# Moving the last conditioning groups of a two-layer encoder from the K/V projections into the first feed-forward

## The chip, the cores and the metric

The kernel runs on one core of one Trainium2 chip. The metric is device time: microseconds from the start of the program on the core to its end. The chip has five engines that run their own instruction streams in order and meet at semaphores: TensorE (PE) multiplies matrices, VectorE (DVE) and GpSimd (POOL) do elementwise work and reductions, ScalarE (ACT) does activations, casts and copies, SyncE (SP) mainly starts DMAs. DMAs move data between the chip's memory and the on-chip buffer.

## The reference

The program is a trunk of two layers over one sequence of 1024 tokens with 1024 channels, everything in float32. Each layer has a mixer and a SwiGLU feed-forward; the first mixer is a gated short convolution, the second is forgetting attention over a shared K/V set. A vector `c` conditions every sub-layer:

```
c_act = silu(c)
for l in 0, 1:
    sh1, sc1, g1, sh2, sc2, g2 = split(c_act @ w_ada[l] + b_ada[l], 6)
    h = x * (1 + sc1) + sh1
    y = short_conv_mixer(h)                     # layer 0
    # layer 1: k, v, gates = shared_kv(x, c, w_ada_kv, b_ada_kv)   (2 more vectors of c)
    #          y = forgetting_attention(h, w_q, k, v, gates, w_o)
    x = layer_norm(alpha * x + g1 * y)
    h = x * (1 + sc2) + sh2
    y = (silu(h @ w_gate) * (h @ w_up)) @ w_down       # inner width 2816
    x = layer_norm(alpha * x + g2 * y)
```

So 14 conditioning vectors of 1024 numbers are needed: six of each layer and two for K and V. Each is the product of one vector with a 1024 by 1024 matrix. The matrices hold some 59 MB.

## The kernel before

**Precision and tiles.** Every large product is made of three passes on PE: a float32 operand is split into a rounded high part (ACT, a cast) and the rest (DVE, a subtraction), and high x high, high x low and low x high are added up (`mm3`, lines 169 to 171). A pass is one matmul of a 128 by 128 weight tile with a 128 by 512 tile.

**The conditioning groups.** A vector is computed in two groups of 512 columns, 24 groups without the first two vectors, which are done at the start. A group needs 1024 rows by 512 columns of weights. DVE adds them up, one step for 128 rows: the first step is a multiplication (`ada_step`, line 260), the other seven multiply and add into one accumulator `ga` (line 262). Then PE transposes the accumulator in four pieces (`ada_finish`, line 285), DVE reduces them (line 287) and adds the bias (line 278). The work is done at three places:

- 8 groups during the convolution (`ada_pump`, weights by POOL's DMA queue).
- 10 groups during the first feed-forward's first phase (`ada_lq`, `ada_slot`). A group is cut into *quarters*: one DMA of 512 KB by SP's queue (line 763) into a page of the common pool, and two DVE steps. One quarter is done in each slot (below).
- 6 groups beside the K and V projections (`ada_item`). Again in quarters; the DMA is issued by POOL (line 807), into the one page lent for it, and an item first does the quarter that was loaded and then asks for the next. What is left after the last K product is done in a loop before the Q products start (`while self.adaq or self.adan or self.adap`).

**The feed-forward's first phase** (`hidden`) computes silu(h w_gate) * (h w_up) with seven products M1 to M7 instead of eight for each pair of 128-column blocks (a fast matrix multiplication of two by two blocks). A *slot* is one such product: 24 matmuls on PE. Sums of weight blocks that M5, M3 and M7 need are made by POOL (lines 898 to 903). In a slot the next slot's weights are split (ACT line 639, DVE line 640), the product runs, and its two banks are evacuated by DVE and ACT (lines 942, 957 to 988), which also forms the inputs of the second phase and stores them.

There are 77 slots in the first phase: slots 0 to 11 are M1 and M2 of pairs 0 to 5, and lie beside the end of a layer norm; from slot 12 on the other five products of pairs 0 to 5 follow, five slots a pair (*early pairs*); from about slot 41 pairs 6 to 10 follow with seven slots each (*late pairs*). Evacuating an early pair adds a part that was put aside in memory, so DVE has more to do there.

**What sets the order.** Loads stand in one list in the order of use (`queue`), and are started from its head while more than a reserve of pages of the common pool is free (`lq_pump`; the reserve is 5 pages there). The call `queue(2, len(slots), ...)` in `run` puts one quarter of conditioning weights behind the blocks of each slot `i >= nada`, with `nada = nfirst + ADA0` and `nfirst = 12`. `adaq_lq(n)` takes `n` groups for that and leaves the others to `ada_item`. The loop in `run` calls `ada_slot` after each slot `i >= nada`. A scheduler then sets the order of instructions on each engine from this; instructions of one engine may change places where the data allow it.

Before the change `ADA0` is 22, so quarters begin in slot 34, and 10 groups, 40 quarters, fill slots 34 to 73.

Of the kernel before, what the change touches and what calls it, by code (L numbers as in the profile page):

```python
# [77 lines left out]
class Builder:  # L78
# [734 lines left out]
    def hidden(self, l, nearly, left):  # L813
# [7 lines left out]
        slots = [(j, n) for j in early for n in ("M1", "M2")]  # L821
        nfirst = len(slots)
        nada = nfirst + ADA0
        late = None
# [27 lines left out]
        def m1_load(j):  # L852
            def fn():
                pg = self.fpage()
                nc.sync.dma_start(pg.rearrange("p a b -> p (a b)"), self.dr["m1"][j * P:(j + 1) * P])
                return pg
            self.lq_add(("m1", j), fn)

        def b11_load(j):
            def fn():  # L860
                pg = self.fpage()
                nc.sync.dma_start(pg[:, 0], self.dr["M1"][j * P:(j + 1) * P])
                return pg
            self.lq_add(("b11", j), fn)
# [3 lines left out]
        def queue(lo, hi, ada):  # L868

            for i in range(lo, hi):  # L870
                for q in [look + i] if i else range(look + 1):
                    if q < len(slots):
                        j, n = slots[q]
                        load(("e" if j in early and n in ("M1", "M2") else "", j, *src[n]))
                if i + look + 1 < len(slots):
                    j, n = slots[i + look + 1]
                    for b in needs.get(n, ()):
                        load(("", j, *b))
                j, n = slots[i]
                if j in early and n == "M5":  # L880
                    m1_load(j)
                if j in early and n == "M3":
                    b11_load(j)
                if i >= nada and ada:
                    self.lq.append(ada.pop(0))
            assert not ada

        def load(key):
            if key not in queued:
                queued.add(key)  # L890
                self.blocks_load(l, key[1], [key[2:]], key[0])
# [167 lines left out]
        def steps(i):  # L1059
            def begin():  # L1060
                self.slot = i
                ahead(i)
            out = [begin]
            if i < nfirst:
                out.append(lambda: self.lq_pump(FRES + 3 * self.sums_left))
            for m in range(2):
                out += [lambda m=m: product(i, m), lambda m=m: evac(i, m)]
            return out + [lambda: self.flush(i)]
# [5 lines left out]
                parts(i)  # L1074

        def run(beside, before_end):
            queue(2, len(slots), self.adaq_lq(len(self.adaq) - 6) if l == 0 else [])
            self.down_queue()
            first = [f for i in range(nfirst) for f in steps(i)]
            self.weave((first, 0.0, 1.0), (beside, *LNE))  # L1080
            for i in range(nfirst, len(slots)):
                self.lq_pump(FRUN if i < len(slots) - 12 else FRUN + 2)
                if i == len(slots) - 2:
                    before_end()
                for f in steps(i):
                    f()
                if i >= nada and l == 0:
                    self.ada_slot()
            self.flush()
            assert not self.adal  # L1090
# [932 lines left out]
FRUN = 5  # L2023
FDOWN = 18
LNE = (0.05, 1.0)
ADA0 = 22
LOOK = 1
FILL = (0,)*5+(2,)*4+(1,)*16
QB_ORDER = (6, 7, 0, 1, 2, 3, 4, 5)
# [33 lines left out]
```

## Time and profile before

| | us |
|---|---|
| median of 3 runs | 2443.26 (2442.11 to 2446.3) |
| the profiled execution | 2442.01 |
| its span in the profile | 2440.2 |
| PE busy in the span | 2320.7 (95%) |
| DVE busy | 1767.6 (72%) |
| POOL busy | 814.3 (33%) |
| first feed-forward, first phase, slots 12 to 73 | 495.5 to 837 |
| K, V, gates, first half of Q | about 1081 to 1342 |

The profile counts the time in which an engine executes. Matmul ends are modelled and matmuls overlap, so a row of PE that is busy all the time says that it never waited; how fast it went is read from the count of matmuls and the granted clock (PEclk: 1.00 is 2.4 GHz, 0.5 would be 1.2 GHz). Times in the windows are microseconds from the start of the span. The views name code by its line (L262 is line 262) and tiles by their names: `ga` is the accumulator of a group, `pg` any page of the pool, `mm` and `sm` banks for results of PE, `tA` and `tB` short-lived tiles.

### The profile page before, as it was taken

The page shows a single profiled execution, that of the slowest core. Times are in us where ns is not written, and L with a number is a line of the kernel's source. Part 1 is how long each engine was busy: PE and PEld are TensorE (multiplying, and loading weights), DVE is VectorE, ACT ScalarE, POOL GpSimd, SP SyncE. Part 2 cuts the span into 40 slices and gives each one's busy share as a digit, 9 for nine tenths or more (in the row PEclk, how much of TensorE's full clock was granted, in tenths as well). Part 3 has the DMA queues.
Part 4 walks back from the last instruction along what each step waited for, and adds up shares of the span by engine and source line. Part 5 has one row for each costly group of instructions (what it writes and reads, how often), then busy time and mean ns, then how long its engine had stood idle before and what let it go on. Part 6 is the DMA issues. An engine that isn't in the chain of part 4 may idle for free. (4 is left out here: it accounts for less than half of the span.)

```text
span 2440.2 us, 29980 instructions
## 1 busy us (share of the span) xinstructions
PE 2320.7 (95%) x10629; PEld 1885.4 (77%) x10629; DVE 1767.6 (72%) x2382; ACT 929.6 (38%) x1423; POOL 814.3 (33%) x664
## 2 busy tenths in 40 slices
PE   7899999999999899999989999999999999999987
PEld 5688887788888788777777777777778888878876
DVE  6665548988988878986474567888787865577973
ACT  3311113622233343434222566666462233333432
POOL 6411003343222323343100465565443322231314
PEclk9999999999999999999999999999999999999998
DMA  8343213555666855115658565563374443374401
GB/s 277 96 129 121 87 36 112 182 185 172 225 198 211 301 173 167 58 52 198 193 183 241 157 189 153 134 161 97 104 244 156 160 130 117 116 272 134 164 1 69
DMA packets 322762, 375.42 MB, mean 154 GB/s; under 512 B 20053, under 2 KB 214821, under 8 KB 322613
## 3 DMA queue, kind: packets, MB, share of 16 engines
q1 hardware_dynamic: 302260, 318.25, 42.1%
q0 software_dynamic: 8736, 29.89, 4.0%
q10 hardware_dynamic: 11616, 25.37, 2.8%
q8 instruction: 84, 1.38, 0.2%
q14 instruction: 66, 0.53, 0.1%
HBM read 288.83 MB, written 84.61 MB: 153 GB/s over the span
## 5 line engine op out<-in xcount | busy, mean ns | idle before, releaser
L169 PE MATMUL mm<-pg,pg 128*128 128x512 f32 x2872 | 1138.7, 398 | 36.3 <-DVE pg L1306 11.1
L170 PE MATMUL mm<-pg,pg 128*128 128x512 f32 x2872 | 1133.3, 395 | 8.5 <-DVE pg L373 6.9
L171 PE MATMUL mm<-pg,pg 128*128 128x512 f32 x2872 | 1130.6, 394 | 6.2 <-POOL pg L371 4.0
L169 PEld LDWEIGHTS mm<-pg,pg 128*128 128x128 f32 x2872 | 546.8, 190 | 158.0 <-DVE pg L1306 14.8
L170 PEld LDWEIGHTS mm<-pg,pg 128*128 128x128 f32 x2872 | 546.7, 190 | 123.6 <-DVE pg L373 10.0
L171 PEld LDWEIGHTS mm<-pg,pg 128*128 128x128 f32 x2872 | 545.9, 190 | 123.2 <-POOL pg L371 5.3
L640 DVE TENSOR_TENSOR pg<-pg,pg 128x1024 fp32r<-128x1024 f32 (+1 forms) x322 | 464.7, 1453 | 96.4 <-ACT pg L639 51.4
L639 ACT CAST pg<-pg 128x1024 fp32r<-128x1024 f32 (+1 forms) x322 | 320.1, 1013 | 515.4 <-PE mm L171 163.6
L1174 POOL TENSOR_TENSOR pg<-pg,pg 128x1024 f32<-128x1024 f32 (+1 forms) x48 | 121.9, 2547 | 271.6 <-DVE pg L640 125.1
L1306 DVE SCALAR_TENSOR_TENSOR pg<-mm,mods,pg 128x512 f32<-128x512 f32 x184 | 134.8, 744 | 60.9 <-PE mm L171 60.7
L159 ACT CAST pg<-pg 128x1024 fp32r<-128x1024 f32 x78 | 81.5, 1052 | 210.5 <-PE mm L170 147.5
L1725 POOL TENSOR_SCALAR pg<-pg,st 128x512 f32<-128x512 f32 (+7 forms) x128 | 97.7, 772 | 116.7 <-DVE st L1723 108.9
L262 DVE SCALAR_TENSOR_TENSOR ga<-pg,cact,ga 128x512 f32<-128x512 f32 x112 | 95.4, 852 | 43.1 <-DMA pg<-in_w_ada_dram 39.1
L1748 DVE TENSOR_TENSOR pg<-sm,pg 128x512 fp32r<-128x512 f32 x192 | 104.0, 550 | 24.2 <-ACT pg L1747 21.3
L901 POOL TENSOR_TENSOR pg<-pg,pg 128x1024 f32<-128x1024 f32 x22 | 55.9, 2540 | 172.4 <-DMA pg<-in_ffn_w_up_dram 93.6
L960 ACT ACTIVATE tA<-tA 128x512 f32<-128x512 f32 x66 | 41.7, 631 | 184.3 <-DVE tA L959 184.3
L1747 ACT CAST pg<-sm 128x512 fp32r<-128x512 f32 x192 | 89.1, 480 | 49.2 <-PE sm L1744 45.6
L1722 ACT ACTIVATE pg<-s,st 128x512 f32<-128x512 f32 (+7 forms) x128 | 94.5, 744 | 28.8 <-DVE st L1719 19.2
L316 POOL DMA_DIRECT2D g<-in_w_ada_dram x64 | 34.8, 543 | 204.9 <-DVE ga L262 76.5
L1716 DVE TENSOR_REDUCE st<-s 128x1 f32<-128x1024 f32 (+3 forms) x96 | 91.2, 951 | 15.2 <-PE s L1710 14.5
L163 DVE TENSOR_TENSOR pg<-pg,pg 128x1024 fp32r<-128x1024 f32 x58 | 72.5, 1257 | 40.0 <-ACT pg L159 39.2
L898 POOL TENSOR_TENSOR pg<-pg,pg 128x1024 f32<-128x1024 f32 x22 | 54.6, 2484 | 139.8 <-DMA pg<-in_ffn_w_up_dram 106.3
(217 smaller groups left out, 2542.4 us busy)
## 6 DMA issues: line engine op xcount, KB each, us to landing
scr_hid<-pg SPq DMA_DIRECT2D x154, 256.0 KB
pg<-scr_hid SPq DMA_DIRECT2D x70, 512.0 KB
pg<-in_ffn_w_gate_dram SPq DMA_DIRECT2D x112, 256.0 KB
pg<-in_ffn_w_up_dram SPq DMA_DIRECT2D x112, 256.0 KB
pg<-in_ffn_w_down_dram SPq DMA_DIRECT2D x88, 256.0 KB
pg<-in_w_ada_dram SPq DMA_DIRECT2D x40, 512.0 KB
g<-in_w_ada_dram POOLq DMA_DIRECT2D x64, 256.0 KB, 3.1
pg<-in_conv_w_in_dram SPq DMA_DIRECT2D x24, 512.0 KB
```

Source lines behind the costliest of these rows:

```text
L169: mm(out, lhsT=whi, rhs=xhi, start=first, stop=False, skip_group_check=skip)
L170: mm(out, lhsT=whi, rhs=xlo, start=False, stop=False, skip_group_check=skip)
L171: mm(out, lhsT=wlo, rhs=xhi, start=False, stop=last, skip_group_check=skip)
L262: eng.scalar_tensor_tensor(acc, w, s, acc, op0=ALU.mult, op1=ALU.add)
L639: nc.scalar.copy(hi[:, 0:n], flat[:, 0:n])
L640: nc.vector.tensor_tensor(lo[:, 0:n], flat[:, 0:n], hi[:, 0:n], op=ALU.subtract)
L1174: tt = lambda o, a, b, op=ALU.subtract: gp.tensor_tensor(o, a, b, op=op)
L1306: nc.vector.scalar_tensor_tensor(z, bank, gate[:, k:k + 1], z, op0=ALU.mult, op1=ALU.add)
L1716: nc.vector.tensor_reduce(m, p[:, :, 0:n], axis=AX.X, op=ALU.min)
L1722: nc.scalar.activation(lg[:, i], p[:, i, 0:n], AF.Exp, bias=m[:, i:i + 1], scale=-1.0, accum_out=s[:, i:i + 1])
L1725: nc.gpsimd.tensor_scalar(lg[:, i], lg[:, i], s[:, i:i + 1], 1.0, op0=ALU.mult, op1=ALU.mult)
L1748: nc.vector.tensor_tensor(pt[:, 1, a:], p[:, a:], pt[:, 0, a:], op=ALU.subtract)
```

## The change

The list of the first phase takes all groups that are left, 16 instead of 10, and quarters begin in slot 12 instead of slot 34. So 64 quarters lie in slots 12 to 75, and the last group is finished in slot 76. No group is left for `ada_item`: its calls beside K and V find nothing to do, and the loop before the Q products is empty.

```diff
@@ hidden(), run @@
         def run(beside, before_end):
-            queue(2, len(slots), self.adaq_lq(len(self.adaq) - 6) if l == 0 else [])
+            queue(2, len(slots), self.adaq_lq(len(self.adaq)) if l == 0 else [])
             self.down_queue()
@@ constants @@
 LNE = (0.05, 1.0)
-ADA0 = 22
+ADA0 = 0
 LOOK = 1
```

Each number of instructions stays: 24 DMAs of 512 KB go from POOL's queue to SP's, and 48 DVE steps, 24 transposes, 6 reductions and 6 bias additions move from the K/V stage to the first phase. All quarters from the first one on stand 22 slots earlier than they did.

On DVE, in the middle of an early pair of the first phase (the end of M7, then M5 and M4), the order before is this; no conditioning step stands there:

```order
L959 TENSOR_TENSOR tA_4184<-mm_700_4091,pg_4029 128x512
L979 TENSOR_TENSOR pg_4199<-mm_702_4106,pg_4029 128x512
L980 TENSOR_TENSOR pg_4199<-pg_4199,tA_4184 128x512
L640 TENSOR_TENSOR pg_4246<-pg_4122,pg_4245 128x1024
L988 TENSOR_TENSOR pg_4199<-pg_4199,pg_4083 128x512
L942 TENSOR_TENSOR pg_4226<-mm_718_4213,pg_4125 128x512
L988 TENSOR_TENSOR pg_4083<-pg_4199,pg_4083 128x512
L942 TENSOR_TENSOR pg_4226<-mm_720_4228,pg_4125 128x512
L640 TENSOR_TENSOR pg_4283<-pg_4008,pg_4282 128x1024
L959 TENSOR_TENSOR tA_4262<-mm_700_4091,pg_3928 128x512
```

At the same place of another early pair the change has this order:

```order
L942 TENSOR_TENSOR pg_4305<-mm_739_4292,pg_4239 128x512
L988 TENSOR_TENSOR pg_4274<-pg_4274,pg_4185 128x512
L262 SCALAR_TENSOR_TENSOR ga_4233<-pg_4241,cact_99,ga_4233 128x512
L988 TENSOR_TENSOR pg_4185<-pg_4274,pg_4185 128x512
L942 TENSOR_TENSOR pg_4305<-mm_741_4307,pg_4239 128x512
L262 SCALAR_TENSOR_TENSOR ga_4233<-pg_4241,cact_99,ga_4233 128x512
L640 TENSOR_TENSOR pg_4327<-pg_4236,pg_4326 128x1024
L262 SCALAR_TENSOR_TENSOR ga_4233<-pg_4282,cact_99,ga_4233 128x512
L959 TENSOR_TENSOR tA_4343<-mm_716_4152,pg_4006 128x512
L262 SCALAR_TENSOR_TENSOR ga_4233<-pg_4282,cact_99,ga_4233 128x512
L640 TENSOR_TENSOR pg_4372<-pg_4141,pg_4371 128x1024
L979 TENSOR_TENSOR pg_4274<-mm_718_4167,pg_4006 128x512
```

Two conditioning steps a slot now stand between the evacuations (L942, L959, L979, L988) and the splits that the next products need (L640).

On DVE at the end of the K products the order before has the last group's steps between the evacuations of K (L1483) and the modulated input of Q (L369, L373):

```order
L163 TENSOR_TENSOR pg_9460<-pg_9457,pg_9459 128x1024
L1483 TENSOR_TENSOR tB_9448<-mm_1573_9422,tA_9447 128x512
L262 SCALAR_TENSOR_TENSOR ga_9356<-pg_9420,cact_99,ga_9356 128x512 x2
L1483 TENSOR_TENSOR tB_9489<-mm_1580_9463,tA_9488 128x512
L262 SCALAR_TENSOR_TENSOR ga_9356<-pg_9455,cact_99,ga_9356 128x512 x2
L287 TENSOR_REDUCE mods_101<-sm_9527 128x4
L1483 TENSOR_TENSOR tB_9522<-mm_1583_9496,tA_9521 128x512
L278 SCALAR_TENSOR_TENSOR mods_101<-mods_101,bada_192 128x4
L369 TENSOR_SCALAR tB_9536<-pg_6172,v_1499_9003,mods_101 128x512
```

With the change the same place reads:

```order
L163 TENSOR_TENSOR pg_9469<-pg_9466,pg_9468 128x1024
L1483 TENSOR_TENSOR tB_9461<-mm_1575_9435,tA_9460 128x512
L1483 TENSOR_TENSOR tB_9498<-mm_1581_9472,tA_9497 128x512
L1787 CAST mask_9583<-tA_9578 128x128
L1483 TENSOR_TENSOR tB_9529<-mm_1584_9503,tA_9528 128x512
L369 TENSOR_SCALAR tB_9536<-pg_6304,v_1514_9068,mods_101 128x512
```

The steps, the reduction and the bias are gone there, and the cast of attention's mask has moved up.

## Rows read from the trace of the kernel before

**Rows 1.** PE's waits from 1075 to 1300: total us, times, longest.

```profile
PE sm L285 <- DVE ga L262: 13.2, 4, 4.6
...
PE sm L1577 <- DVE pg L1570: 3.4, 1, 3.4
```

**Rows 2.** Stretches, K/V stage: busy us of PE, PEld, DVE, ACT, POOL; PEclk.

```profile
1130.00:1180.00 50.00, 48.60 (x219) 39.97 (x218) 22.00 (x31) 11.66 (x16) 4.19 (x6) 1.00 0.65 204
1198.00:1208.00 10.00, 7.14 (x28) 4.34 (x27) 5.28 (x7) 3.28 (x4) 0.72 (x1) 0.83 0.64 193
1262.00:1274.00 12.00, 7.63 (x29) 5.88 (x28) 9.37 (x17) 1.53 (x2) 1.44 (x2) 0.86 0.51 167
1291.00:1302.00 11.00, 6.43 (x25) 5.08 (x24) 5.62 (x11) 5.28 (x8) 1.45 (x3) 0.84 0.98 277
```

**Rows 3.** Same view: slots 12-15, five early pairs, two late pairs, the phase's end.

```profile
495.50:517.30 21.80, 21.80 (x98) 18.06 (x97) 16.53 (x16) 5.26 (x6) 14.56 (x6) 1.00 0.69 203
517.30:544.50 27.20, 27.20 (x122) 22.52 (x121) 23.55 (x23) 6.94 (x8) 10.36 (x5) 1.00 0.53 169
544.50:571.70 27.20, 27.20 (x122) 22.52 (x121) 23.11 (x23) 6.95 (x8) 10.18 (x5) 1.00 0.51 164
571.70:598.90 27.20, 27.20 (x122) 22.52 (x121) 23.23 (x23) 6.96 (x8) 10.13 (x5) 1.00 0.53 165
598.90:626.10 27.20, 27.20 (x122) 22.52 (x121) 22.94 (x28) 6.76 (x8) 4.03 (x2) 1.00 0.66 216
626.10:653.70 27.60, 27.60 (x125) 22.87 (x124) 26.46 (x33) 7.60 (x10) 7.54 (x3) 1.00 0.70 220
692.80:731.80 39.00, 39.00 (x177) 32.29 (x176) 32.99 (x44) 13.74 (x19) 11.16 (x5) 1.00 0.61 196
731.80:770.40 38.60, 38.60 (x174) 31.94 (x173) 33.60 (x39) 13.01 (x17) 10.30 (x4) 1.00 0.62 198
837.10:862.60 25.50, 19.20 (x78) 15.36 (x77) 24.01 (x18) 9.88 (x12) 17.27 (x6) 0.87 0.83 313
```

**Rows 4.** Same view, second feed-forward: a late pair without conditioning.

```profile
2005.90:2044.00 38.10, 38.10 (x170) 31.55 (x169) 19.66 (x21) 12.97 (x17) 9.55 (x4) 1.00 0.33 104
```

**Rows 5.** Conditioning steps, 604 to 843: min/median/max ns, first and last start.

```profile
L262 DVE SCALAR_TENSOR_TENSOR ga<-pg,cact,ga x70: 734/751/2953, 609.6 to 826.7; 128x512 f32<-128x512 f32 x70
...
L260 DVE TENSOR_SCALAR ga<-pg,cact x10: 475/478/1984, 609.0 to 818.8; 128x512 f32<-128x512 f32 x10
```

**Rows 6.** By shape, DVE, 698.2 to 814.9: busy us, mean ns, idle before.

```profile
L287 DVE TENSOR_REDUCE mods<-sm 128x4 f32<-128x512 f32 x5 | 3.4, 687 | 5.1 <-PE sm L285 5.1
L278 DVE SCALAR_TENSOR_TENSOR mods<-mods,bada 128x4 f32<-128x4 f32 x5 | 3.0, 595 | 0.0
```

**Rows 7.** By shape, three early pairs, 517.3 to 598.9.

```profile
L640 DVE TENSOR_TENSOR pg<-pg,pg 128x1024 fp32r<-128x1024 f32 x16 | 31.6, 1974 | 5.4 <-PE mm L170 5.4
...
L942 DVE TENSOR_TENSOR pg<-mm,pg 128x512 f32<-128x512 f32 x12 | 8.2, 682 | 1.3 <-PE mm L171 1.3
...
L903 POOL TENSOR_TENSOR pg<-pg,pg 128x1024 f32<-128x1024 f32 x3 | 7.2, 2411 | 6.2 <-DVE pg L640 6.2
```

**Rows 8.** By shape, late pairs of the second feed-forward, 2005.9 to 2120.1.

```profile
L640 DVE TENSOR_TENSOR pg<-pg,pg 128x1024 fp32r<-128x1024 f32 x21 | 25.6, 1221 | 18.6 <-ACT pg L639 18.6
```

**Rows 9.** In order of time, DVE, 646.5 to 656: start, us.

```profile
655.61 2.88 DVE L262 SCALAR_TENSOR_TENSOR ga<-pg,cact,ga 128x512 f32<-128x512 f32 x1
```

**Rows 10.** In order of time, POOL, 646.5 to 656.

```profile
655.23 2.71 POOL L901 TENSOR_TENSOR pg<-pg,pg 128x1024 f32<-128x1024 f32 x1 [1.24 <-DVE pg L640]
```

**Rows 11.** PE's waits at the end of the first phase, 837.1 to 862.6.

```profile
PE mm L169 <- DVE tA L959: 6.3, 1, 6.3
```

**Rows 12.** POOL's waits in the three early pairs, 517.3 to 598.9.

```profile
POOL pg L901 <- DMA pg<-in_ffn_w_up_dram: 28.6, 3, 9.6
POOL pg L898 <- DMA pg<-in_ffn_w_up_dram: 16.1, 3, 5.6
```

**Rows 13.** DMA issues: count, KB each, median us from issue to landing.

```profile
pg<-in_w_ada_dram POOLq DMA_DIRECT2D x24, 512.0 KB, 4.6
```

## The prediction

> **What bounds the kernel now.** I read the windows by stage first: in slots 12 to 73 of the first phase the PE column is as long as the stretch, in every row at full granted clock [rows 3]. There PE never waits, and nothing that is taken off another engine saves time. The waits of PE come next: in the K/V stage it waits 13.2 us in four pieces for conditioning steps (a transpose of `ga` behind line 262), and 3.4 us once for the gates [rows 1]. So the groups beside K and V sit on the path that sets the end. The question is what the first phase pays to take them, and the engine to look at is DVE: 23.1 to 23.6 us busy of 27.2 in an early pair without any conditioning, and some 33 of 39 in a late pair with seven quarters [rows 3].
>
> **What is saved beside K and V.** Three terms.
> - The four waits: 13.2 us [rows 1].
> - The clock behind them. The stretch 1130 to 1180 holds one short wait (48.6 of 50 us busy) and has 1.00. The three stretches around the other waits have 0.83, 0.86 and 0.84 [rows 2]; PE had idled before each fall, and the missing part is time at 1.2 instead of 2.4 GHz. If a part of 0.17 of 10 us is lost, and 0.14 of 12 and 0.16 of 11, this is 1.7 + 1.7 + 1.8 = 5.1 us.
> - The transposes. A late pair with two groups finished in it takes 39.0 us, one without 38.1 [rows 3, 4], so a group costs PE 0.45 us; six cost 2.7.
>
> Together 21.0 us. It can be less: a wait can return behind the next instruction, and the wait for the gates [rows 1] does not go, since PE's work between the gates' product and their transposes stays. From below I take 13 us (the waits alone), from above 22. POOL's queue loses 24 DMAs there; nothing that PE waited for stood behind them except those groups, so I cost this at nothing. SP's queue takes them, in the first phase.
>
> **What the first phase pays.** The transposes come back there: 2.7 us, since PE has no gap to put them in.
>
> DVE is the large term. A quarter's price first. From above: a late pair holds 33.0 and 33.6 us of DVE with seven quarters and 19.7 without any [rows 3, 4], so (33.3 - 19.7) / 7 = 1.95 us a quarter. By its instructions alone: a group is one first step, seven others, a reduction and a bias, at 0.478, 0.751, 0.687 and 0.595 us [rows 5, 6], 7.02 us or 1.75 a quarter. From below: the early pairs at 598.9 to 653.7 already hold quarters 1 to 7 of the old order, with 22.9 + 26.5 = 49.4 us of DVE; two pairs without them would have 2 x 23.3 = 46.6 (mean of three rows), so only 2.8 us came on top, 0.4 a quarter, and PE did not wait [rows 3]. But POOL ran only 11.6 us in those two windows, where two earlier pairs have 20.5 [rows 3]: part of its sums lay elsewhere, and that lightens DVE (below). In the change POOL's sums fall in every early pair. I take 1.75, which lies next to the row from late pairs.
>
> An early pair then needs 23.3 + 5 x 1.75 = 32.05 us of DVE. PE needs 27.2 + 1.25 x 0.45 = 27.8. DVE, in order, is 4.3 us a pair too slow, and the splits for the next product stand in its queue behind the steps, so PE waits for it. Slots 16 to 33 are 3.6 pairs: 15.4 us. Slots 12 to 15 have DVE busy for 16.5 of 21.8 [rows 3]; four quarters make 23.5 against 22.2 for PE: 1.3 us. Slots 34 to 41 held quarters before and I count nothing new. Sum 16.7 us; bounds 0 (at 0.4 a quarter, DVE stays under PE) and 21.1 (at 1.95).
>
> Then the end of the phase. Two more quarters, in slots 74 and 75, and a reduction fall into 837.1 to 862.6, where DVE is busy for 24.0 of 25.5 us [rows 3] and PE waits 6.3 us for it [rows 11]. No cover is left: 2 x 1.75 = 3.5 us; bounds 0 (DVE has idle time just ahead of that stretch, and the scheduler may use it) and 4.
>
> Then the clock. If the 4.3 us of a pair come in one piece, they are like the waits in [rows 2], each followed by some 1.7 us; over four pairs up to 6.8. They will come in pieces of one to three us, so I take half, 3.4.
>
> Loads: the quarters add 512 KB to each slot from 12 to 33. The early pairs move 164 to 169 GB/s, and 313 GB/s were moved at the end of the phase [rows 3]; 512 KB in 5.44 us is 96 GB/s more, so the rate itself is not reached. I take nothing; the other end is a rival below.
>
> **Sum.** -21.0 + 2.7 + 16.7 + 3.5 + 3.4 = +5.3 us. The profiled execution took 2442.0 us, 1.3 below the median of the three runs, and the same sum on the median of 2443.3 gives 2448.6. **I predict 2449 us.** About 0.2% (4.9 us) is what a measurement of this kernel can tell from no change, so this forecast lies just above that edge.
>
> **Rivals.**
>
> *The idle time of DVE swallows the quarters: faster.* The mechanism is elastic time: part of DVE's busy time is being held up by POOL. In three early pairs a split (line 640) takes 1.97 us on average [rows 7], and 1.22 in the second feed-forward's late pairs [rows 8], though the work is the same. If DVE runs its queue without gaps, POOL is the one to wait, as it did at 598.9 to 653.7. For it: the 0.4 us a quarter there. Against it: the late pairs' 1.95, with POOL at 10 to 11 us as ever. It decides below 0.89 us a quarter ((27.8 - 23.3) / 5). Then the DVE term and its clock term are nothing: -21.0 + 2.7 + 3.5 = -14.8, 2428 us.
>
> *POOL's sums shut DVE out for their whole length: slower still.* A step of line 262 that began at 655.61, 0.38 us after a sum of POOL, took 2.88 us against a median of 0.75 and ended when the sum did [rows 5, 9, 10]; it did not run beside it. The Trainium skill says of this (SBUF — State Buffer, section "SBUF: two separate sides") that DVE, with two inputs in the buffer, and GpSimd hold a common pair of ports exclusively for a whole instruction, and the other one is fully blocked; the row just named agrees. Worked out from rows: undisturbed, an early pair is 5 splits of 1.22 and some 16 other instructions of 0.68 [rows 7, 8], 17.0 us, so of POOL's 10.2 us a pair 6.3 now hold DVE up. With a full queue on DVE all four sums of 2.4 us [rows 7] would: 17.0 + 8.75 + 9.6 = 35.4 us a pair, 7.6 too slow, 27.4 over 3.6 pairs. With 1.3, 3.5, and 6.8 of clock: -21.0 + 2.7 + 39.0 = +20.7, 2464 us. Against it: instructions that read results of PE (line 942) show 0.68 us in the midst of this [rows 7] and take up part of a sum's time.
>
> *The look-ahead of loads shrinks.* Per early pair the list holds eleven pages instead of six while the reserve of five pages stays, and one quarter in each pair is loaded in the slot that uses it. POOL already waits 28.6 and 16.1 us for landed weights in three pairs [rows 12], which nobody has to wait for now. If one landing of 512 KB, 4.6 us [rows 13], shows on PE in each of four pairs: 18.4 more than the forecast, 2467 us. Against it: the late pairs run with quarters in the same list and PE shows no wait [rows 3].
>
> **How the numbers follow.** Chances: forecast 0.48 (2443 to 2456 by its own bounds), elastic DVE 0.27, POOL's lock 0.13, look-ahead 0.12. The range 2427 to 2466 holds the forecast, most of the faster case and the lock; beyond it I leave about 0.1 on each side. Faster by over 0.2%: 0.24 from the elastic case and 0.02 of the forecast, 0.26. Within 0.2%: 0.20 of the forecast and 0.06 of the others, 0.26. Slower: 0.26 of the forecast and 0.22 of the two slow cases, 0.48.
>
> **What the profile after would show.** PE's wait for line 262 is gone in the K/V stage, the gates' wait is still there, and that stage is about 21 us shorter. From slot 12 to slot 41 PE shows waits for lines 640 and 959 to 988, some 17 us in all, with DVE busy throughout. If DVE is as busy and PE does not wait, the elastic case holds; if steps of 2.5 us and more are the rule beside sums, the lock does; if DVE or POOL stand idle until a DMA of `w_ada` or `ffn_w_up` and PE waits for them, the look-ahead. I am wrong about the K/V stage if other waits of PE fill the places of the four.

## The result and the profile after

| | before | after |
|---|---|---|
| median, same chip | 2442.69 us (2440.6 to 2446.3) | 2431.78 us (2430.24 to 2433.95) |
| profiled span | 2440.2 | 2429.1 |
| PE busy | 2320.7 | 2316.2 |
| DVE busy | 1767.6 | 1773.5 |

The ratio is 0.995 with a 95% interval of 0.9934 to 0.9966: the change makes the kernel faster by 11 us, where 6 us slower was forecast. The profiled spans, cut at the same places of the program, say where (slot boundaries are starts of PE's matmuls, worked out from the trace; V begins at the first evacuation of V, the last part at the first product of attention):

| us | start to slot 12 | slots 12 to 41 | slot 41 to V | V to attention | rest | span |
|---|---|---|---|---|---|---|
| before | 495.5 | 158.2 | 442.2 | 247.8 | 1096.5 | 2440.2 |
| after | 495.0 | 174.6 | 444.1 | 219.8 | 1095.6 | 2429.1 |
| difference | -0.5 | +16.4 | +1.9 | -28.0 | -0.9 | -11.1 |

First PE's waits in the K/V stage, which lie some 18 us later now; the columns are those of [rows 1].

```profile
PE mm L171 <- POOL pg L371: 3.3, 1, 3.3
PE sm L486 <- POOL rs L481: 1.2, 2, 0.8
PE mm L171 <- DVE pg L373: 0.5, 2, 0.3
PE sm L478 <- DVE acc L473: 0.3, 1, 0.3
```

Nothing of line 262 is left, and the wait for the gates (line 1577, 3.4 us in [rows 1]) is gone with it. The first wait, for line 371 on POOL ahead of V, was 2.9 us before.

What the steps beside K and V waited for themselves is to be seen in the kernel before: DVE's waits from 1165 to 1300 and, in order of time, the last two steps of the group whose transposes PE waited for at 1200.

```profile
DVE ga L262 <- DMA pg<-in_w_ada_dram: 33.3, 10, 7.0
```

```profile
1201.34 1.54 DVE L262 SCALAR_TENSOR_TENSOR ga<-pg,cact,ga 128x512 f32<-128x512 f32 x2 [3.34 <-DMA pg<-in_w_ada_dram]
```

In three of PE's four waits the last steps had waited for their own load in this way. So it is in the main the load into the one lent page, and not a lack of DVE's time, that PE waited for there. A second page beside K and V, which would leave the groups where they are, was not tried.

The granted clock around the gates, before and then after, in the windows' columns of [rows 2]:

```profile
1225.00:1237.00 12.00, 8.61 (x29) 6.64 (x28) 9.28 (x14) 3.31 (x5) 0.72 (x1) 0.72 0.57 173
```

```profile
1225.00:1237.00 12.00, 12.00 (x57) 9.46 (x56) 10.76 (x17) 6.67 (x9) 0.00 (x0) 1.00 0.21 76
```

A mean of 0.72 says that the lower level, 1.2 GHz, held for 6.7 of the 12 us; at half speed this is worth up to 3.4 us (0.28 x 12). It came with PE's wait for the gates.

The first phase after, in the same view as [rows 3]: slots 12 to 15, then five early pairs.

```profile
495.10:516.90 21.80, 21.80 (x98) 18.06 (x97) 16.79 (x20) 4.68 (x6) 7.69 (x3) 1.00 0.83 252
516.90:547.70 30.80, 28.46 (x130) 23.24 (x129) 29.89 (x35) 7.67 (x9) 8.17 (x4) 1.00 0.80 242
547.70:582.00 34.30, 29.47 (x126) 24.05 (x125) 33.71 (x39) 6.94 (x8) 13.11 (x5) 0.95 0.71 227
582.00:609.80 27.80, 27.80 (x126) 22.85 (x125) 27.66 (x33) 6.53 (x7) 11.38 (x4) 1.00 0.72 238
609.80:638.90 29.10, 27.82 (x126) 22.82 (x125) 29.07 (x35) 7.16 (x8) 9.95 (x4) 1.00 0.74 235
638.90:669.70 30.80, 28.73 (x130) 23.14 (x129) 30.42 (x40) 8.03 (x10) 5.25 (x4) 1.00 0.72 227
```

Read the DVE column against the length: idle for 0.9, 0.6, 0.1, 0.0 and 0.4 us in a pair that was idle for some 4 before. DVE has become the engine without a gap, and the pairs last 27.8 to 34.3 us instead of 27.2. PE's waits from 490 to 690:

```profile
PE sm L285 <- DVE ga L262: 6.1, 2, 4.8
PE mm L169 <- DVE pg L942: 3.8, 2, 2.3
PE mm L169 <- DVE tA L959: 0.6, 1, 0.6
```

They are 10.5 us, all for DVE. The transposes wait for the conditioning steps here, as they did beside K and V, and banks wait to be evacuated. Behind the one of 4.8 us (PE idle from 564.99) the clock fell again; DVE in order of time there:

```profile
559.85 2.77 DVE L262 SCALAR_TENSOR_TENSOR ga<-pg,cact,ga 128x512 f32<-128x512 f32 x1
562.55 3.40 DVE L640 TENSOR_TENSOR pg<-pg,pg 128x1024 fp32r<-128x1024 f32 x1
565.87 0.68 DVE L979 TENSOR_TENSOR pg<-mm,pg 128x512 f32<-128x512 f32 x1
566.48 0.74 DVE L262 SCALAR_TENSOR_TENSOR ga<-pg,cact,ga 128x512 f32<-128x512 f32 x1
567.13 0.68 DVE L980 TENSOR_TENSOR pg<-pg,tA 128x512 f32<-128x512 f32 x1
567.74 0.68 DVE L942 TENSOR_TENSOR pg<-mm,pg 128x512 f32<-128x512 f32 x1
568.34 0.67 DVE L988 TENSOR_TENSOR pg<-pg 128x512 f32<-128x512 f32 x1
568.94 0.74 DVE L262 SCALAR_TENSOR_TENSOR ga<-pg,cact,ga 128x512 f32<-128x512 f32 x1
569.60 0.68 DVE L942 TENSOR_TENSOR pg<-mm,pg 128x512 f32<-128x512 f32 x1
```

POOL at the same time:

```profile
559.54 2.53 POOL L898 TENSOR_TENSOR pg<-pg,pg 128x1024 f32<-128x1024 f32 x1 [6.92 <-issue]
562.15 2.72 POOL L899 TENSOR_TENSOR pg<-pg,pg 128x1024 f32<-128x1024 f32 x1
```

Two things are to be seen. A step and a split that meet a sum of POOL take 2.77 and 3.40 us, as in [rows 9, 10]. And in a full queue the next instruction begins 0.65 us after a step of 0.74 (566.48 to 567.13): durations overlap by some 0.08 us, so a sum of durations counts too much.

By shape, 517.3 to 626, against [rows 7]:

```profile
L262 DVE SCALAR_TENSOR_TENSOR ga<-pg,cact,ga 128x512 f32<-128x512 f32 x29 | 30.6, 1056 | 0.1
L640 DVE TENSOR_TENSOR pg<-pg,pg 128x1024 fp32r<-128x1024 f32 x18 | 26.3, 1459 | 1.1 <-ACT pg L639 1.1
...
L942 DVE TENSOR_TENSOR pg<-mm,pg 128x512 f32<-128x512 f32 x14 | 9.4, 677 | 0.0
```

The splits (1.97 before) are shorter, the steps longer than their 0.75: the sums of POOL now fall on the steps as well. Line 942, which reads results of PE, keeps its 0.68.

At the end of the phase and in the second phase, PE's waits from 840 to 1075:

```profile
PE mm L169 <- DVE tA L959: 4.2, 1, 4.2
PE mm L169 <- DVE pg L1306: 3.3, 2, 2.6
PE mm L170 <- DVE pg L640: 2.8, 1, 2.8
```

The first was 6.3 us [rows 11]; the third was 0.6, and the clock behind it is low now:

```profile
886.00:896.00 10.00, 7.24 (x27) 5.52 (x26) 7.36 (x5) 1.09 (x2) 3.16 (x2) 0.83 0.94 305
```

### The profile page after: what moved, and what is told of

It is laid out like the page before. It is cut to its first block, busy times and chain, and to the rows that moved or that the text cites. A ratio compares the mean times of both kernels' runs of the same rounds, so it can differ in the third digit from the quotient of the medians.

```text
span 2429.1 us, 29994 instructions
## 1 busy us (share of the span) xinstructions
PE 2316.2 (95%) x10629; PEld 1881.2 (77%) x10629; DVE 1773.5 (73%) x2382; ACT 930.5 (38%) x1423; POOL 799.9 (33%) x640
## 5 line engine op out<-in xcount | busy, mean ns | idle before, releaser
L169 PE MATMUL mm<-pg,pg 128*128 128x512 f32 x2872 | 1136.6, 397 | 39.7 <-DVE pg L1306 11.1
L640 DVE TENSOR_TENSOR pg<-pg,pg 128x1024 fp32r<-128x1024 f32 (+1 forms) x322 | 454.6, 1421 | 84.3 <-ACT pg L639 50.5
L1748 DVE TENSOR_TENSOR pg<-sm,pg 128x512 fp32r<-128x512 f32 x192 | 104.0, 551 | 26.6 <-ACT pg L1747 23.8
L262 DVE SCALAR_TENSOR_TENSOR ga<-pg,cact,ga 128x512 f32<-128x512 f32 x112 | 111.3, 994 | 1.3
```

What stands on the lines that cost most here:

```text
L169: mm(out, lhsT=whi, rhs=xhi, start=first, stop=False, skip_group_check=skip)
L262: eng.scalar_tensor_tensor(acc, w, s, acc, op0=ALU.mult, op1=ALU.add)
L640: nc.vector.tensor_tensor(lo[:, 0:n], flat[:, 0:n], hi[:, 0:n], op=ALU.subtract)
L1748: nc.vector.tensor_tensor(pt[:, 1, a:], p[:, a:], pt[:, 0, a:], op=ALU.subtract)
```

## Experiments

The theory after the result had three parts: the whole gain is that of the K/V stage, the gates' wait included; the price is paid in the early pairs by DVE's steps; POOL's sums decide how full DVE is. Rivals: the gain comes from elsewhere (loads moved off POOL's queue, the order of later stages), or the price is one of loads. Medians are set beside the kernel before on the same chip; the stages are those of one profiled execution each. Two profiled executions of the same kernel differ by 0.1 to 0.5 us in slots 12 to 41, by up to 1.7 from slot 41 to V (444.1 and 445.8 for the change) and by up to 4.2 in the rest (1094.8 and 1099.0 for the version with one group left from slot 16). The stages of the profiled runs:

| us | slots 12 to 41 (PE idle) | slot 41 to V | V to attention | rest | median, ratio to before (95%) |
|---|---|---|---|---|---|
| groups left out | 158.2 (0) | 441.2 | 221.2 | 1094.3 | 2412.54, 0.9863 (0.9842 to 0.9884) |
| early start only | 175.1 (10.7) | 441.1 | 251.2 | 1098.0 | 2464.15, 1.0073 (1.0053 to 1.0094) |
| loads only | 161.9 (0.5) | 448.9 | 220.6 | 1100.7 | 2427.71, 0.9915 (0.9889 to 0.9942) |
| steps only | 172.2 (7.0) | 442.9 | 221.1 | 1100.0 | 2430.85, 0.9934 (0.9915 to 0.9954) |
| small sums | 161.2 (0.0) | 449.4 | 221.3 | 1094.8 | 2419.28, 0.9884 (0.9861 to 0.9906) |
| after, once more | 174.7 (8.0) | 445.8 | 220.9 | 1095.5 | 2434.53, 0.9955 (0.9937 to 0.9972) |
| one left, from slot 16 | 168.9 (6.5) | 441.5 | 221.5 | 1094.8 | 2422.86, 0.9912 (0.9895 to 0.9928) |
| one left, spread | 160.5 (0.3) | 449.1 | 221.1 | 1095.7 | 2424.99, 0.9915 (0.9897 to 0.9932) |
| two left, from slot 20 | 165.8 (4.4) | 446.2 | 227.3 | 1097.5 | 2433.32, 0.9944 (0.9928 to 0.9961) |
| one left, spread late | 169.4 (6.4) | 446.5 | 222.6 | 1099.0 | 2429.33, 0.9926 (0.9910 to 0.9942) |

**The groups beside K and V left out** of the kernel before:

```diff
-        self.adaq, self.adan, self.adaa = self.adaq[n:], None, 0
+        self.adaq, self.adan, self.adaa = [], None, 0
```

> The order of before, with the six groups beside K and V left out altogether (their vectors are zero, so layer 1 has no conditioning). This prices the K/V stage alone. My theory: all of that stage's gain, 27.9 us from line 371's wait to attention's first scores, came from taking DVE's conditioning steps out of it, the wait for the gates (line 1577, 3.4 us and its half clock) too; so the stage is again about 232 us instead of 260, the first phase is as before (slots 12 to 41 in 158 us), and the total is about 2415 us. Rival, the working of the prediction: the gates' wait belongs to the order of PE's own work, and went only because the first phase moved something; then the wait stays, the stage is about 239 us and the total about 2422 us.

The vectors that are left out are set to zero by POOL at the start; else nothing is changed. The K/V stage takes 221.2 us against 247.8, so the groups cost 26.6 us there. The wait for the gates is 1.2 us. The other stretches differ by 0 to 2.2 us: the gain belongs to the stage. It does not tell the steps from their loads, since both are left out.

**The early start alone**: `ADA0` is 0, six groups stay beside K and V.

```diff
-ADA0 = 22
+ADA0 = 0
```

> Only ADA0 is 0; the six groups stay beside K and V, so 40 quarters lie in slots 12 to 51 and none in slots 52 to 75. Theory: the price is paid by the early pairs alone; slots 12 to 41 take about 174 us as in the changed kernel, slots 52 to 74 run a little faster than before (five groups' transposes less, 2 us), the K/V stage stays at 260 us: total 2442.7 + 16 - 2 = about 2457 us. Rival: the price comes from the list being longer as a whole (pages held, the end of the phase); then slots 12 to 41 take about 160 us and the total is within 5 us of before.

Slots 12 to 41 take 175.1 us, as in the change, and the K/V stage keeps its waits (251.2, 3.4 more than before, which was not expected). The total is 18 us above the kernel before, where 14 were expected. The price belongs to the early pairs, and is paid without any gain for it.

**Loads or steps.** Once the change with all loads, but steps on 64 of 512 columns, and once with full steps on one page that is loaded once:

```diff
-            self.ada_step(self.gacc, w[:, i], 2 * a + i, self.nc.vector)
+            n = HALF if a == i == 0 else 64
+            self.ada_step(self.gacc[:, 0:n], w[:, i, 0:n], 2 * a + i, self.nc.vector)
```

> The changed kernel with all its loads and pages, but the conditioning steps of the first phase work on 64 of 512 columns (all but the first of a group), so the vectors are wrong and DVE is relieved of most of the work. Theory, DVE is the bound in slots 12 to 41: they take 159 to 161 us instead of 174.5, the total is 2431.8 - 14 = about 2418 us. Rival, the loads and the shorter look-ahead are the bound: the slots stay at 172 to 175 us, total about 2431 us.

```diff
-        w = self.lq_get(("ada", j, a))
-        self.ada_quarter(j, a, w)
-        self.lq_drop(("ada", j, a))
+        if self.ada_w is None:
+            self.ada_w = self.fpage((P, 2, HALF))
+            self.nc.sync.dma_start(self.ada_w, self.ada_cols(j, 4)...[:, 0:2])
+        self.ada_quarter(j, a, self.ada_w)
...
-        return [self.ada_lq(j, a) for j, a in self.adal]
+        self.ada_w = None
+        return []
```

> The changed kernel with all its conditioning steps, but every quarter of the first phase reads one page that is loaded once, so 63 of 64 loads of 512 KB are left out (the vectors are wrong) and the list of loads holds weights of the feed-forward alone. Theory, DVE is the bound: slots 12 to 41 take 170 to 176 us and the total is within 5 us of 2432. Rival, loads and look-ahead: the slots fall to 158 to 162 us and the total to about 2418 us. If part of each holds, slots between 162 and 170 us.

The loads alone leave 161.9 us, 3.7 over before (2.7 of it transposes by the forecast's price); the steps alone 172.2. So of the 16.4 us the steps pay most. But the loads are not free elsewhere, and their total is 2427.7 where about 2418 was expected: with them the stretch from slot 41 to V takes 448.9 instead of 442.2, and the new wait behind the phase (line 640, 2.8 us) is there; with the steps alone it is not. That wait comes with the loads.

**POOL's sums on 16 of 128 columns** in the first feed-forward's first phase, else the change:

```diff
-            g = lambda r, c: self.lq_get(("", j, r, c))
+            g = lambda r, c: self.lq_get(("", j, r, c))[:, :, :, 0:16 if l == 0 else P]
```

> The changed kernel, with the first feed-forward's sums of weight blocks on POOL (lines 898 to 903) done for 16 of 128 columns only, so that POOL is busy for a small part of its 10 us a pair; the rest of each sum is left out and everything else, all conditioning steps included, stays. My theory (DVE is short of time there through its own instructions and partly through POOL holding them up): DVE at 17.0 + 8.75 = 25.8 us a pair comes under PE's 27.8, so slots 12 to 41 take about 161 us instead of 174.6, and the kernel about 2418. If the splits of line 640 take 1.97 us for a reason of their own (the rounded output, not POOL), slots 12 to 41 stay at 172 to 175 us and the kernel at 2431.

PE does not wait in slots 12 to 41 at all, with all quarters in them (against the change 3.4 us more are saved ahead of slot 12, where sums fall too, and 5.3 go again from slot 41 to V). The windows' row from 517.3 to 626.1, and two groups by shape:

```profile
517.30:626.10 108.80, 108.80 (x491) 90.08 (x490) 94.66 (x140) 27.51 (x32) 8.15 (x16) 1.00 0.81 258
```

```profile
L262 DVE SCALAR_TENSOR_TENSOR ga<-pg,cact,ga 128x512 f32<-128x512 f32 x35 | 26.8, 766 | 2.7 <-DMA pg<-in_w_ada_kv_dram 1.5 <-DMA pg<-in_w_ada_dram 1.1
L640 DVE TENSOR_TENSOR pg<-pg,pg 128x1024 fp32r<-128x1024 f32 x20 | 24.5, 1224 | 8.0 <-PE mm L170 4.6 <-PE mm L171 1.7 <-POOL pg L901 1.2
```

The split is back at 1.22 us, the step at 0.77: nothing but POOL's sums stretched them. DVE is busy for 94.7 us in 3.93 pairs of 27.7, 24.1 a pair with five quarters. The change has (29.89 + 33.71 + 27.66 + 29.07) / 4 = 30.1, so the sums hold DVE up for 6.0 us a pair, of 10.7 that POOL is busy there.

**The gates.** From the kernel before, the item ahead of the gates done later:

```diff
-                self.ada_item()
+                if f != 2:
+                    self.ada_item()
```

> The kernel before, with the one conditioning item beside the third K product (just ahead of the gates) skipped, so that it is done later with the others; no work is left out. If the gates' wait (3.4 us at line 1577) comes from conditioning steps that stand ahead of the gates' evacuation on DVE, it falls to the 1.2 us or less that it had without any groups beside K and V. If it is the gates' own chain, as my prediction said, it stays at 3.4. The four waits for the accumulator stay in both cases, so the total is 2436 to 2443 in the one and 2442 in the other.

There is one run: 2449.67 us beside 2441.28 to 2452.3 of before, and the wait stays at 3.5. It does not settle the question, because the order moved another item into the same place. DVE between the gates' evacuations:

```profile
1219.25 0.73 DVE L262 SCALAR_TENSOR_TENSOR ga<-pg,cact,ga 128x512 f32<-128x512 f32 x1
...
1220.25 0.73 DVE L262 SCALAR_TENSOR_TENSOR ga<-pg,cact,ga 128x512 f32<-128x512 f32 x1
...
1226.78 0.73 DVE L262 SCALAR_TENSOR_TENSOR ga<-pg,cact,ga 128x512 f32<-128x512 f32 x1
...
1227.78 0.73 DVE L262 SCALAR_TENSOR_TENSOR ga<-pg,cact,ga 128x512 f32<-128x512 f32 x1
...
1231.24 1.27 DVE L1570 TENSOR_TENSOR_SCAN pg<-zero,pg,tA 16x512 f32<-16x512 f32 x1
```

Four steps, 2.9 us, stand inside the gates' chain; before has the same four. From the gates' last product to the end of the scan of line 1570 it is 16.6 us in before and 17.8 here. In the change, its second run, the groups left out, the small sums and the versions with one and two groups left, no step lies in the chain: 12.7 to 14.2 us (worked out from their traces), and the wait is 0 to 1.4. With the early start alone the four steps stand there and the chain takes 18.2. So the wait goes when the steps go, also where a group is still done beside K and V.

**Other splits of the work**, with no work left out, and the change itself on the same chip:

> The changed kernel once more, as the measure for the other versions on the same chip: 2431.8, with slots 12 to 41 at 174 to 175 us.

One group left beside K and V and quarters from slot 16 on:

```diff
-            queue(2, len(slots), self.adaq_lq(len(self.adaq)) if l == 0 else [])
+            queue(2, len(slots), self.adaq_lq(len(self.adaq) - 1) if l == 0 else [])
...
-ADA0 = 0
+ADA0 = 4
```

> No work left out. One group stays beside K and V and quarters begin in slot 16. The four quarters in slots 12 to 15 lie beside DVE work of 16.5 of 21.8 us, where the theory has them nearly free; so against the changed kernel this saves at most 1.3 us there, and the group beside K and V costs 0 to 4: 2430 to 2435. If instead the quarters in slots 12 to 15 are what starts the trouble in the pairs behind them (a backlog on DVE that is carried on), slots 16 to 41 get shorter by some 5 us and the total is 2425.

2422.86 against 2434.53 us of the change on this chip, and the intervals of their ratios do not meet: less than the change, and the lowest median of the versions with all the work. The K/V stage stays at 221.5 (220.9 in the change), so the first group there costs next to nothing, and slots 12 to 41 pay 168.9, 5.8 less than the change there. The second of the expectations was right: without quarters in slots 12 to 15 the pairs behind them get shorter, not those slots (21.8 us in both). Another 4.3 us lie between slot 41 and V (441.5 against 445.8) and are not explained. Run again on another chip it gave 2427.56 (0.992, 0.9904 to 0.9937), over what was expected:

> One group left beside K and V and quarters from slot 16 on, once more, as the measure for the version above on the same chip: 2420 to 2425.

Two groups left, from slot 20 on (`- 2`, `ADA0 = 8`):

> No work left out. Two groups stay beside K and V and quarters begin in slot 20, so eight of the early pairs' quarters are gone. My theory: the early pairs pay for 14 new quarters instead of 22, slots 12 to 41 about 167 us, and the eight items left beside K and V lie ahead of the gates' evacuation; the last of them may give back one wait of 3 to 4 us with its clock. Total 2421 to 2429. The rival, that each group beside K and V costs its share of the 28 us, gives 9 us back there: 2431 to 2434.

The early pairs pay 165.8 and the second group beside K and V costs 6 us (227.3; PE waits 2.4 us for line 262 once). The total, 2433.3, is a draw with the change, over the range of my theory and inside the rival's; but the rival's share, 9 us for two groups, is not what the stage shows, nothing for the first group and 6 for the second.

Quarters spread by a table that gives the number for each slot, once by DVE's idle time and once with more of them late:

```diff
-                if i >= nada and ada:
+                for _ in range(ADAC.get(i, 0) if ada else 0):
                     self.lq.append(ada.pop(0))
...
-                if i >= nada and l == 0:
+                for _ in range(ADAC.get(i, 1 if i > 73 else 0) if l == 0 else 0):
                     self.ada_slot()
```

> No work left out. 15 groups in the first phase, the last one beside K and V ahead of the gates; the 60 quarters stand where DVE has time by the rows: three in slots 12 to 15, two for each pair in slots 16 to 30, one a slot from 34 on with two more for each late pair, none in slots 74 and 75. My theory (each stage pays only for what goes beyond DVE's free time): slots 12 to 41 take 159 to 162 us, slots 41 to 74 183 to 188, the second phase 239 as before, the K/V stage about 221, sum about 2415 to 2420. If what counts is the number of quarters outside the K/V stage, wherever they stand, it keeps at least nine tenths of what the change paid in slots 12 to 41: 2429 to 2431.

> No work left out. One group stays beside K and V; of the 60 quarters three stand in slots 12 to 15, eleven in slots 16 to 33 (18 in the version with one group left and quarters from slot 16 on), one in each slot from 34 to 75, and four more in the fifth and sixth late pairs' slots 57 to 67. My theory (an early pair has room for some three quarters with POOL's sums beside it): slots 12 to 41 take 160 to 163 us against 168.9, the K/V stage 221.5, the stretch from slot 41 to V 442 to 446; total 2416 to 2420. If what DVE does not pay in the early pairs it pays at the phase's end, as the loads that come late there let it seem (the two variants with light early pairs had some 7 us more from slot 74 on), the gain is given back: 2421 to 2424.

The first does in slots 12 to 41 what it should, 160.5 us, and gives back 7 us between slot 41 and V: 2425, over the 2415 to 2420 expected, and not to be told from the version with quarters from slot 16 on (the intervals lie on each other). The second misses: 169.4 in slots 12 to 41, and a median of 2429.3, over both of its ranges (the profiled execution is its slowest, 2435.1). There a step waits for its own quarter's load, and DVE with all behind it; whether PE's 6.4 us of idle come from this was not tried. DVE's waits from 575 to 690:

```profile
DVE ga L262 <- DMA pg<-in_w_ada_kv_dram: 3.5, 3, 1.9
DVE pg L640 <- ACT pg L639: 0.9, 2, 0.6
```

and behind the phase, PE's waits from 860 to 930:

```profile
PE mm L170 <- DVE pg L640: 7.6, 2, 4.9
```

So counting DVE's idle time alone does not make a good table: loads and what follows the phase have to be counted too.

## Why the prediction was wrong

The forecast had the sign wrong. The mechanism was right in outline on both sides: the waits beside K and V went, the early pairs became bound by DVE, and PE waited there, though not for what was named (6.1 us for transposes behind line 262 and 4.4 for lines 942 and 959, none for the splits of line 640). The sum was wrong by 16.4 us: 7.0 beside K and V, 6.4 in slots 12 to 41, 1.6 from slot 41 to V and 1.4 in stretches that I had put at nothing.

- **"The wait for the gates does not go"** failed. I read it as the gates' own chain and did not look at what stands inside that chain on DVE. Four steps of line 262 do. The stage gave 28.0 us instead of 21.0; the difference is the wait of 3.4 and up to 3.4 of clock. Leaving the groups out takes away 2.2 of the wait and all of the clock's loss (1.00 over the stage) without the rest of the change.
- **"A quarter costs 1.75 us", and so 16.7 us of waiting** was too much. PE waited 10.5 us. The price was a sum of mean durations, and two things made it too high. On a full queue a step costs 0.65, not 0.75, so ten instructions a group cost some 0.08 us less each. And the 0.595 us of line 278 in [rows 6] is no price of that instruction; the same five, as min/median/max in ns:

```profile
L278 DVE SCALAR_TENSOR_TENSOR mods<-mods,bada x5: 153/159/2349, 706.6 to 796.7; 128x4 f32<-128x4 f32 x5
```

Alone it takes 0.16 us, and one of the five, which stood beside a sum of POOL, took 2.35. So the price held a share of POOL's sums without saying so. With 0.16 a group is 6.58 us, and a quarter (6.58 - 0.8) / 4 = 1.45 us. Slots 16 to 33 and 34 to 40 show the price as measured, before and then after:

```profile
517.30:615.20 97.90, 97.90 (x434) 81.06 (x433) 83.46 (x84) 24.53 (x28) 31.62 (x13) 1.00 0.54 172
615.20:653.70 38.50, 38.50 (x173) 31.90 (x172) 35.82 (x43) 10.67 (x13) 10.61 (x4) 1.00 0.70 226
```

```profile
516.90:628.00 111.10, 102.64 (x454) 83.93 (x453) 109.46 (x129) 24.52 (x28) 37.13 (x14) 0.98 0.72 227
628.00:669.70 41.70, 39.63 (x178) 32.17 (x177) 41.28 (x50) 11.82 (x14) 10.73 (x6) 1.00 0.77 251
```

DVE has 26.0 us more for the 18 quarters of slots 16 to 33, 1.44 each, with 5.5 us more of POOL beside them. At 1.45 a pair needs 23.3 + 7.25 = 30.55 us, 2.75 more than PE, 9.9 us over 3.6 pairs; PE idles for 8.5 there. The stretch of slots 34 to 40 was put at nothing because it held quarters before, and that failed too: it takes 3.2 us more, of which 2.1 are waiting. The four quarters of slots 12 to 15, at 1.3 us in the forecast, cost nothing in their place: DVE has 16.79 of 21.8 us there with them, as POOL has 7.69 instead of 14.56; but the version from slot 16 on shows 5.8 us less in the pairs behind. By what way they are handed on is open; that some of POOL's sums move from slots 12 to 15 into those pairs is one possibility. The clock was put at 3.4 us and cost 1.7 (0.95 over 34.3 us). The small sums, with the same transposes and without a wait, take 3.0 more than before, so the transposes' 2.7 is near. Some 1.2 of the 16.4 us are not accounted for. In the second run of the change the slots take 174.7 us with 8.0 of waiting and some 5 of clock (0.97 over the stretch): the sum is firmer than its parts.
- **"Then the end of the phase, 3.5 us"** failed. The wait fell from 6.3 to 4.2. The versions with steps alone and with small sums have the same two quarters there and wait 6.1 and 6.4, so the quarters cost nothing there, the lower bound that I had named. Why the change itself waits 2 us less is not settled; the kernel with the groups left out, whose first phase is that of before, waits 4.1 as well, so these 2 us need not come from the change. The new wait of the second phase gives it back: from slot 41 to V it is +1.9 in all, where 3.5 were forecast.

The terms as they came out: -28.0 + 16.4 + 1.9 - 1.4 = -11.1.

The rivals: that idle time on DVE swallows the quarters is refuted (PE waits 10.5 us, and DVE is idle for 2.0 us in five pairs), though its total, 2428, lies nearest; that is luck, since it is made of other terms (-14.8 = -21.0 + 2.7 + 3.5). That POOL's sums shut DVE out for their whole length does not hold as a sum: 6.0 of 10.7 us a pair, against 6.3 of 10.2 that I read before the change (a low figure, since it too counts durations). A full queue did not make the hold longer. The single instruction does behave like that: the step and the split at 559.85 and 562.55 end with the sums or after them. The Trainium skill's rule (SBUF — State Buffer, section "SBUF: two separate sides") says that DVE with two inputs in the buffer and GpSimd shut each other out for a whole instruction; these two rows agree. Line 942, which reads PE's results, kept its 0.68 us meanwhile. And yet the sums are what makes DVE too slow: without them there is no wait. The look-ahead was a small part: the steps without loads take 2.4 us less in slots 12 to 41.

## What to carry to other kernels

When work is moved off a stage, look at every chain in that stage for instructions of it, not only at the waits that name it; the wait for the gates named another line. On a queue without gaps, price an instruction by the distance of starts, not by its duration, and take the median of an instruction and not a mean that another engine has stretched. The split with the lowest median left the one group that cost next to nothing where it was, and a stage's free time must be counted with its loads and with POOL's sums, which hold DVE up.

## What the runs showed of the hardware

- DVE instructions of 0.74 and 0.68 us follow each other at 0.60 to 0.66 us.
- With POOL's sums in the stretch the same split took 1.46 us on average (up to 3.40), and 1.22 with the sums cut to 16 columns; a step 1.06 and 0.77. A 128x4 instruction of 0.16 us took 2.35 beside a sum.
- A wait of PE was followed by a low clock in one place and not in another: 2.8 us of idle at 888.76 and 0.83 over the 10 us around it, 2.3 us of idle in the pair from 516.9 and 1.00. In the second run of the same kernel 2.6 us of idle at this second place was followed by a low clock too (0.89 over 530 to 545). What decides was not tried.
